# Weight casts behind the output gate's copies, a written TensorE order for the inverse and attention's output products, and query scaling on ScalarE

## The chip, the cores and the metric

One core of one Trainium2 chip runs the whole program. The time is the device time of one execution in microseconds (us). Of the kernel before there are three timed runs and one profiled execution, whose records the profile and the trace show.

## The reference, cut to what matters

One encoder layer on 512 tokens of width 1024: a feed-forward half step, a token mixer of two head groups, a second feed-forward half step, each behind an RMS norm with scale and shift from a condition vector. The change lies in the mixer:

```python
proj = h @ w_in                                    # q, k, v, z of the delta group; latents of attention
qkv = silu(causal_conv(concat(gq, gk, gv)))        # 4 taps
# gated delta rule, chunks of 64, per head:
M = I + where(strict, beta * (k k^T) * decay, 0)   # unit lower triangular
W = triangular_solve(M, [v * beta, k * beta * exp(G)])
# recurrence over chunks with a state S, then
o_a = rms(o_a) * norm_w * silu(gz)                 # the output gate z
# latent attention, 4 heads, block-causal:
q_nope = rms(q_nope) * w * scale ;  q_rope = rope(rms(q_rope)) * scale
o_b = rms(softmax(q k^T) v) * norm_w
x = x + gate2 * (concat(o_a, o_b) @ w_out)
```

All is float32. The dense products are each made of three products of two rounded parts: high x high, high x low, low x high.

## The kernel before

Activations lie feature-major, in eight tiles of 128 features x 512 tokens, each as a high and a low part. A weight unit is 128 output features x 1024 inputs. It is loaded by a DMA that SyncE issues (`load`, L118), cast to its high part on ScalarE (L193) and subtracted to its low part on VectorE (L198). There are four buffers for each of raw, high and low parts. `next_unit` (L260) prepares a unit ahead of the one that it hands out. `dense` (L270) makes, for each of eight input tiles, three products of 512 columns (L266 to L268) into one of three accumulators in PSUM (`psa`); all other products use five more PSUM tiles (`psb`).

A scheduler that works at compile time orders the instructions of each engine. It takes them by program order where its own model of time has their inputs ready, so an instruction can be placed ahead of one written before it. Each engine then works through its list in order and waits at an instruction whose inputs or buffers aren't ready. The code can pin an order: `follow` (L128) puts one instruction behind another on its engine, and `matmuls_in_order` (L144) chains all TensorE instructions of a block except those marked loose.

The mixer (L1909) interleaves generators. `Side.step` advances one of its open generators to its next `yield`. Three sides exist: `chain` (lifting the latents, keys of the delta rule, base blocks, inverses, solves), `deltas` (query parts of the delta rule) and `att` (preparing queries and keys, attention by 128-query blocks and head pairs). `dense_units` (L1208) runs four dense units each for k, q, v and the gate z and steps the sides between them. Each unit ends in a `finish`: for z a copy on ScalarE from the accumulator (L1921), later passed through SiLU.

The parts that the change and the prediction touch:

- `prep_q` (L1730): sums of squares of the queries, reciprocal roots (L182 to L189), rotary part on VectorE (L1206 `qrx`, L1830 to L1834, result `qro`), transposes on TensorE (L1768). Then eight GpSimd multiplications scale the other query part in place (L1776, recorded at L1206 as `upo`), and four transposed head tiles follow (L1725).
- `base_blocks` (L1492): 16x16 diagonal blocks of the inverse by substitution on VectorE, with two round trips through DRAM whose DMAs are in SyncE's queue beside the weight loads.
- `inverse` (L1533), one generator for each of four token blocks of 128: two steps of 128x128 products (L1553, L1559), two steps of 32x32 products in two halves j = 0 and 64 (L1569 with copies L1571, L1577 with L1579), a transposition (L1587), and two steps of 64x64 products (L1592, L1598).
- `solve` (L1605) uses an inverse; `recur` (L1637) carries the state through the four blocks; `gated_out` (L1681) norms and gates a block and writes the delta heads' tiles of `mixed`; `attended` (L1887) writes an attention head's tile of `mixed` (high part L1905, low part L1906).
- `out_attended` (L2036): the output projection's half that belongs to attention, for each of eight output tiles four slices, one for each head, of three products of 512 columns.
- The loop at L1992 runs until the second solve and `deltas` are done. It steps `chain` twice, `deltas` once, attention (`rest`) four times and, once attention is through, one slice of `out_attended` (`fill`). No order is pinned there. The loop over `recur` behind it already stands inside `matmuls_in_order`, with chain and attention loose.

Behind the mixer comes the second feed-forward step, in a pinned order.

Of the kernel before, what the change touches and what calls it, by code (L numbers as in the profile page):

```python
# [14 lines left out]
AF = mybir.ActivationFunctionType  # L15
# [3 lines left out]
P = 128  # L19
# [60 lines left out]
class Block:  # L80
# [1124 lines left out]
    def mul(self, out, a, b, eng=None):  # L1205
        (eng or self.nc.vector).tensor_tensor(out=out, in0=a, in1=b, op=ALU.mult)  # L1206

    def dense_units(self, n, side, steps, finish):  # L1208
        for i in range(n):
            u, p = self.next_unit(), self.acc()  # L1210
            for k in range(0, 8, 2):
                self.dense(p, u, self.h, k0=k, k1=k + 2)
                side.step(steps)
            finish(i, p)

    def latents(self, nb):

# [315 lines left out]
    def inverse(self, p):  # L1533

        nc = self.nc
        h4 = lambda x: x.rearrange("p (h d) -> p h d", h=4)
        hs = lambda h: slice(h * P, (h + 1) * P)
        at = self.at[p]

        def flip(src):  # L1540

            t = self.slot(s="T")
            nc.vector.transpose(out=t, in_=src)
            return t

        t = self.slot(s="t0")
        self.mul(t.rearrange("p (h i c) -> p h i c", h=4, i=8),
                 self.t16[:, 4 * p:4 * p + 4, :].unsqueeze(2).to_broadcast([P, 4, 8, 16]),
                 self.dmask.rearrange("p (i c) -> p i c", i=8).unsqueeze(1).to_broadcast([P, 4, 8, 16]))
        u = flip(t)  # L1550
        py = self.aux()
        for h in range(4):
            nc.tensor.matmul(py[:, hs(h)], at[:, hs(h)], t[:, hs(h)], start=True, stop=True)  # L1553
        y = self.slot(s="Y")
        self.mul(h4(y), h4(py), self.lmask.unsqueeze(1).to_broadcast([P, 4, P]))
        yield
        pz = self.aux()
        for h in range(4):
            nc.tensor.matmul(pz[:, hs(h)], y[:, hs(h)], u[:, hs(h)], start=True, stop=True)  # L1559
        un = self.slot(s="U")  # L1560
        nc.vector.tensor_tensor(out=un, in0=u, in1=pz, op=ALU.subtract)
        t = flip(un)
        yield

        py, y = self.aux(), self.slot(s="Y")
        for j in (0, 64):
            a, b = slice(j, j + 32), slice(j + 32, j + 64)
            for h in range(4):
                nc.tensor.matmul(py[b, 32 * h:32 * h + 32], at[a, h * P + j + 32:h * P + j + 64],  # L1569
                                 t[a, h * P + j:h * P + j + 32], start=True, stop=True, tile_position=(j, j + 32))  # L1570
            nc.scalar.copy(y[b, :P], py[b, :P])  # L1571
        yield
        pz = self.aux()
        for j in (0, 64):
            a, b = slice(j, j + 32), slice(j + 32, j + 64)
            for h in range(4):
                nc.tensor.matmul(pz[a, 32 * h:32 * h + 32], y[b, 32 * h:32 * h + 32],  # L1577
                                 un[b, h * P + j + 32:h * P + j + 64], start=True, stop=True, tile_position=(j + 32, j))
            nc.vector.tensor_scalar(out=h4(un[a, :])[:, :, j + 32:j + 64],  # L1579
                                    in0=pz[a, :P].rearrange("p (h c) -> p h c", h=4), scalar1=-1.0, scalar2=None,  # L1580
                                    op0=ALU.mult)
        yield

        a, b = slice(0, 64), slice(64, P)
        pt, t = self.aux(), self.slot(s="T")
        for h in range(4):
            nc.tensor.transpose(pt[a, 64 * h:64 * h + 64], un[a, h * P:h * P + 64], self.ident[a, a])  # L1587
        nc.scalar.copy(t[a, :256], pt[a, :256])
        yield
        py, y = self.aux(), self.slot(s="Y")  # L1590
        for h in range(4):
            nc.tensor.matmul(py[b, 64 * h:64 * h + 64], at[a, h * P + 64:h * P + P], t[a, 64 * h:64 * h + 64], start=True,  # L1592
                             stop=True, tile_position=(0, 64))
        nc.scalar.copy(y[b, :256], py[b, :256])
        yield
        pz = self.aux()
        for h in range(4):
            nc.tensor.matmul(pz[a, 64 * h:64 * h + 64], y[b, 64 * h:64 * h + 64], un[b, h * P + 64:h * P + P], start=True,  # L1598
                             stop=True, tile_position=(64, 0))
        nc.vector.tensor_scalar(out=h4(un[a, :])[:, :, 64:], in0=pz[a, :256].rearrange("p (h c) -> p h c", h=4),  # L1600
                                scalar1=-1.0, scalar2=None, op0=ALU.mult)
        yield
        self.inv[p] = un
# [77 lines left out]
    def gated_out(self, p):  # L1681

        nc = self.nc
        ss = self.small(4, "gs")
        self.head_squares(self.o[p], ss)
        ve = self.small(4, "ve")
        nc.vector.scalar_tensor_tensor(out=ve, in0=ss, scalar=1.0 / P, in1=self.oe[:, 4 * p:4 * p + 4], op0=ALU.mult,
                                       op1=ALU.add)
        r = self.rsqrt(ve, 4)
        yield  # L1690
        on = self.head_scale(self.o[p], r)
        yield
        j = self.vcol["gdn_norm_w"]
        pt = self.aux()
        for h in range(4):
            nc.tensor.transpose(pt[:, h * P:(h + 1) * P], on[:, h * P:(h + 1) * P], self.ident)
        m = self.slot(s="mf")
        ts = slice(p * P, (p + 1) * P)
        for h in range(4):
            hs = slice(h * P, (h + 1) * P)  # L1700
            mh, ml = self.mixed[h]
            nc.vector.scalar_tensor_tensor(out=m[:, hs], in0=pt[:, hs], scalar=self.cwT[:, j:j + 1],
                                           in1=self.zT[h][:, ts], op0=ALU.mult, op1=ALU.mult)
            nc.scalar.copy(mh[:, ts], m[:, hs])
            nc.vector.tensor_tensor(out=ml[:, ts], in0=m[:, hs], in1=mh[:, ts].bitcast(F32), op=ALU.subtract)
        yield

    def head_squares(self, o, ss):
# [21 lines left out]
    def prep_q(self, q):  # L1730

        nc = self.nc
# [3 lines left out]
        for b in range(NB):  # L1736
            for g in range(2):
                c = 6 * (2 * b + g)
# [11 lines left out]
        rqn, rqr = r[:, :16], r[:, 16:]  # L1750
# [21 lines left out]

        for b in range(NB):
            for g in range(2):
                qv = q[b][g][:, :384].rearrange("p (h d) -> p h d", h=2)[:, :, :128]
                self.mul(qv, qv, self.bc(rqn[:, 4 * b + 2 * g:4 * b + 2 * g + 2], 2), nc.gpsimd)  # L1776
        yield
        for h in range(4):
            c = (h % 2) * 192
# [129 lines left out]
    def mixer(self, nb):  # L1909
# [8 lines left out]

        def z_done(i, p):
            z = self.slot(s="z")  # L1920
            nc.scalar.copy(z, p)  # L1921
            self.zT.append(z)

        def conv_done(ct0, dst):
            def f(i, p):
# [6 lines left out]

        self.inv = [None] * NB
        self.kd, self.us, self.o, self.wk = ([None] * NB for _ in range(4))
        self.S = None

        def prepared():
            self.qrT, self.qnT, self.knT = [], [], []
# [36 lines left out]
                yield  # L1975

        chain.add(solving())
        self.dense_units(4, Rates(sides, (1, 0.75, 2)), 1, z_done)
        silu(self.zT)
        accum = self.slot(s="na")  # L1980

        fill = Side()
# [6 lines left out]

        rest = Side(wide=3)  # L1990
        rest.add(others())
        while self.wk[1] is None or deltas.open or deltas.todo:  # L1992
            chain.step(2)
            deltas.step()
            rest.step(4)
            if not rest.open and not rest.todo:
                fill.step(1)

        def loosely(side, n):
            with self.traced() as block:  # L2000
                side.step(n)
            self.loose.update(i.name for i in block)

        na = self.norm_half(0, accum, 6, True)
        self.mixed[:4] = [(self.slot(F32R, "mh"), self.slot(F32R, "ml")) for _ in range(4)]
        with self.matmuls_in_order():
            gated = Side(wide=NB)
            for p in range(NB):
                while self.wk[p] is None:
                    loosely(chain, 1)  # L2010
                for _ in self.recur(p):
                    loosely(chain, 2)
                    loosely(rest, 4)
                    if not rest.open and not rest.todo:
                        fill.step(3)
                    gated.step(2)
                gated.add(self.gated_out(p))
                gated.step()
                if p == 1:
                    def half():  # L2020
                        while len(gated.todo) + len(gated.open) > 2:
                            yield
                        yield from self.out_half(0, accum)
                    fill.add(half())
            while rest.open or rest.todo:
                loosely(rest, 1)
            fill.step(4)
            gated.flush()
            fill.flush()
            self.new_h()  # L2030
            self.tm = [self.slot(s="tm") for _ in range(KT)]
            drain(self.out_half(1, accum, na))
            drain(na)
# [72 lines left out]
```

## Time and profile before

| what | us |
|---|---|
| median of 3 runs | 1079.23 |
| lowest, highest | 1076.95, 1079.45 |
| the profiled execution | 1077.71 |
| its span, first to last instruction | 1076.0 |
| mean granted TensorE clock | 0.987 |

In the rows of the trace, a window row has for each engine its busy us and, in brackets, the number of instructions, then the granted TensorE clock as a share of full speed, the share of time in which the DMA engines worked, and GB/s. A timeline row has start and duration in us, the engine, the line of the kernel, the operation and what it writes and reads; in square brackets stands how long the engine was idle before it and what ended that. A float32 product of 128 or fewer columns appears as two records. PE is TensorE, DVE VectorE, ACT ScalarE, POOL GpSimd, SP SyncE.

### The profile page before, as it was taken

The numbers are of one execution on the slowest core, as the hardware profiler recorded it, in microseconds if no ns is written. First come the engines' busy times: TensorE is split into PE (matmuls) and PEld (weight loads), VectorE is DVE, ScalarE is ACT, GpSimd is POOL, SyncE is SP. The second block draws the span as 40 slices with busy tenths as digits, with TensorE's granted clock in tenths as the row PEclk, the third lists the DMA queues.
The fourth block names the chain that finished last, engine by engine and source line by source line (L and its number), as shares of the span: only waits on it lengthen the run. The fifth ranks groups of instructions, "written<-read, shape, count | busy, mean of one in ns | idle before, by whom it ended". The sixth has DMA issues, their size and how long they took to land. (4 is left out here: it accounts for less than half of the span.)

```text
span 1076.0 us, 15659 instructions
## 1 busy us (share of the span) xinstructions
PE 1046.7 (97%) x6183; PEld 899.1 (84%) x6183; DVE 689.4 (64%) x1231; ACT 445.3 (41%) x761; POOL 51.3 (5%) x103
## 2 busy tenths in 40 slices
PE   6999999999999999998999899999999999999998
PEld 5788878788887898887778578988899999999997
DVE  4488983433577445558868644769768787777633
ACT  3342222222222245566575363465534444444322
POOL 1000000000000011102000030220000000000000
PEclk8999999999999999999999898999999999999999
DMA  9989963233698349411203001153432333233222
GB/s 274 277 240 310 301 203 99 81 98 93 199 289 263 95 120 240 113 49 40 79 25 92 26 21 39 40 126 91 129 107 79 118 115 98 83 118 99 67 71 79
DMA packets 203687, 136.85 MB, mean 127 GB/s; under 512 B 13777, under 2 KB 186590, under 8 KB 203614
## 3 DMA queue, kind: packets, MB, share of 16 engines
q1 hardware_dynamic: 202318, 131.14, 41.1%
q0 software_dynamic: 1296, 4.72, 2.4%
q8 instruction: 48, 0.79, 0.3%
q14 instruction: 25, 0.20, 0.1%
HBM read 128.63 MB, written 2.49 MB: 122 GB/s over the span
## 5 line engine op out<-in xcount | busy, mean ns | idle before, releaser
L266 PE MATMUL pa<-hh,wh 128*128 128x512 f32 (+1 forms) x597 | 227.0, 380 | 4.3 <-ACT z L1921 4.3
L268 PE MATMUL pa<-hh,wl 128*128 128x512 f32 (+1 forms) x597 | 225.0, 377 | 2.7 <-DMA wl<-wr 2.7
L267 PE MATMUL pa<-hl,wh 128*128 128x512 f32 (+1 forms) x597 | 224.8, 377 | 0.0
L193 ACT CAST wh<-wr 128x1024 fp32r<-128x1024 f32 (+1 forms) x106 | 108.0, 1019 | 258.3 <-PE pa L267 184.4
L198 DVE TENSOR_TENSOR wl<-wr,wh 128x1024 fp32r<-128x1024 f32 (+1 forms) x97 | 114.4, 1180 | 99.0 <-ACT wh L193 94.5
L266 PE MATMUL pa<-ah,wh 128*128 128x512 f32 (+1 forms) x396 | 145.5, 367 | 0.6 <-DVE xT L873 0.4
L267 PE MATMUL pa<-al,wh 128*128 128x512 f32 (+1 forms) x396 | 144.5, 365 | 0.0
L268 PE MATMUL pa<-ah,wl 128*128 128x512 f32 (+1 forms) x396 | 143.5, 362 | 0.0
L266 PEld LDWEIGHTS pa<-hh,wh 128*128 128x128 f32 x597 | 113.6, 190 | 27.2 <-ACT z L1921 4.7
L268 PEld LDWEIGHTS pa<-hh,wl 128*128 128x128 f32 x597 | 113.5, 190 | 23.1 <-DMA wl<-wr 3.3
L267 PEld LDWEIGHTS pa<-hl,wh 128*128 128x128 f32 x597 | 113.5, 190 | 19.2 <-DVE hl L453 0.4
L268 PEld LDWEIGHTS pa<-ah,wl 128*128 128x128 f32 x396 | 74.8, 189 | 12.0
L266 PEld LDWEIGHTS pa<-ah,wh 128*128 128x128 f32 x396 | 75.2, 190 | 10.4 <-ACT wh L193 1.7
L267 PEld LDWEIGHTS pa<-al,wh 128*128 128x128 f32 x396 | 75.2, 190 | 7.2
L551 DVE SCALAR_TENSOR_TENSOR aa<-ar,sc,aa 128x512 f32<-128x512 f32 x98 | 73.2, 751 | 9.7 <-DMA ar<-in_w_ada 8.5
L846 PE MATMUL pb<-fh,wh 128*128 128x256 f32 x144 | 40.7, 282 | 0.0
L848 PE MATMUL pb<-fh,wl 128*128 128x256 f32 x144 | 40.7, 283 | 0.0
L848 PE MATMUL pb<-hh,wl 128*128 128x256 f32 x144 | 40.7, 283 | 0.0
L847 PE MATMUL pb<-fl,wh 128*128 128x256 f32 x144 | 40.7, 282 | 0.0
L847 PE MATMUL pb<-hl,wh 128*128 128x256 f32 x144 | 40.7, 282 | 0.0
L846 PE MATMUL pb<-hh,wh 128*128 128x256 f32 x144 | 40.6, 282 | 0.0
L873 DVE SCALAR_TENSOR_TENSOR xT<-pa,mod,xT 128x512 f32<-128x512 f32 (+1 forms) x40 | 29.4, 736 | 17.5 <-PE pa L268 17.5
(433 smaller groups left out, 1995.0 us busy)
## 6 DMA issues: line engine op xcount, KB each, us to landing
wr<-in_ffn_w_in SPq DMA_DIRECT2D x82, 512.0 KB, 4.1
ar<-in_w_ada SPq DMA_DIRECT2D x48, 512.0 KB, 5.9
wr<-in_ffn_w_out SPq DMA_DIRECT2D x34, 512.0 KB, 3.4
ar<-in_w_ada SPq DMA_DIRECT2D x48, 256.0 KB, 4.8
wr<-in_w_in SPq DMA_DIRECT2D x21, 512.0 KB, 3.9
wr<-in_ffn_w_out SPq DMA_DIRECT2D x17, 384.0 KB, 3.4
wl<-wr POOLq DMA_DIRECT2D x9, 512.0 KB, 5.6
wr<-in_w_out SPq DMA_DIRECT2D x8, 512.0 KB, 4.8
```

The costliest lines, as they stand in the source:

```text
L193: self.nc.scalar.copy(hi, raw)
L198: self.nc.vector.tensor_tensor(out=lo, in0=raw, in1=hi.bitcast(F32), op=ALU.subtract)
L266: mm(out, wh, xh, start=start, stop=False)
L267: mm(out, wh, xl, start=False, stop=False)
L268: mm(out, wl, xh, start=False, stop=stop)
L551: nc.vector.scalar_tensor_tensor(out=acc, in0=a, scalar=sc, in1=acc, op0=ALU.mult, op1=ALU.add)
L846: mm(out, wh, xh, start=start and k == 0, stop=False, **kw)
L847: mm(out, wh, xl, start=False, stop=False, **kw)
L848: mm(out, wl, xh, start=False, stop=stop and k == 3, **kw)
L873: nc.vector.scalar_tensor_tensor(out=self.xT[t][:, ts], in0=p[:, ts], scalar=gate[:, t:t + 1], in1=self.xT[t][:, ts], op0=ALU.mult, op1=AL ...
```

## The change

Four edits in the mixer, and one condition that goes with them.

1. For the gate's units, `dense_units` gets `tied=True`. Two units are prepared first. Each later unit is prepared after a gate copy is written, and its instructions on ScalarE (the cast) are pinned behind that copy. This holds the casts of the third and fourth gate unit and of the first two units of the output projection.
2. The loop at L1992 is put inside `matmuls_in_order`, with `deltas` and attention loose. It steps `chain` once a turn and `fill` every second turn, so that one slice of attention's output products stands after every two steps of the inverse, in an order that TensorE keeps.
3. In the inverse's 32x32 steps the two halves alternate product by product, and the two copies come after all eight products.
4. The queries are scaled by sixteen ScalarE activations of 128x128 with a column of factors, instead of eight GpSimd multiplications of 128x256.
5. The output projection's first half starts by a count of gated blocks (`self.gated`) instead of by the number of open generators.

```diff
-    def dense_units(self, n, side, steps, finish):
+    def dense_units(self, n, side, steps, finish, tied=False):
+        if tied:
+            self.prefetch(2)
         for i in range(n):
-            u, p = self.next_unit(), self.acc()
+            u, p = self.ready.pop(0) if tied else self.next_unit(), self.acc()
             for k in range(0, 8, 2):
                 self.dense(p, u, self.h, k0=k, k1=k + 2)
                 side.step(steps)
-            finish(i, p)
+            done = finish(i, p)
+            if tied:
+                with self.traced() as block:
+                    self.prefetch(2)
+                for x in block:
+                    if x.engine == done.engine:
+                        self.follow(x, done.name)
...
         py, y = self.aux(), self.slot(s="Y")
-        for j in (0, 64):
-            a, b = slice(j, j + 32), slice(j + 32, j + 64)
-            for h in range(4):
+        for h in range(4):
+            for j in (0, 64):
+                a, b = slice(j, j + 32), slice(j + 32, j + 64)
                 nc.tensor.matmul(py[b, 32 * h:32 * h + 32], at[a, h * P + j + 32:h * P + j + 64],
                                  t[a, h * P + j:h * P + j + 32], start=True, stop=True, tile_position=(j, j + 32))
+        for j in (0, 64):
+            b = slice(j + 32, j + 64)
             nc.scalar.copy(y[b, :P], py[b, :P])
...
         for b in range(NB):
             for g in range(2):
-                qv = q[b][g][:, :384].rearrange("p (h d) -> p h d", h=2)[:, :, :128]
-                self.mul(qv, qv, self.bc(rqn[:, 4 * b + 2 * g:4 * b + 2 * g + 2], 2), nc.gpsimd)
+                for e in range(2):
+                    qv, c = q[b][g][:, 192 * e:192 * e + P], 4 * b + 2 * g + e
+                    nc.scalar.activation(qv, qv, AF.Copy, scale=rqn[:, c:c + 1])
...
-        self.dense_units(4, Rates(sides, (1, 0.75, 2)), 1, z_done)
+        self.dense_units(4, Rates(sides, (1, 0.75, 2)), 1, z_done, True)
...
-        while self.wk[1] is None or deltas.open or deltas.todo:
-            chain.step(2)
-            deltas.step()
-            rest.step(4)
-            if not rest.open and not rest.todo:
-                fill.step(1)
...
+        with self.matmuls_in_order():
+            turn = 0
+            while self.wk[1] is None or deltas.open or deltas.todo:
+                chain.step(1)
+                loosely(deltas, 1)
+                loosely(rest, 4)
+                turn += 1
+                if not rest.open and not rest.todo and turn % 2:
+                    fill.step(1)
...
-                        while len(gated.todo) + len(gated.open) > 2:
+                        while self.gated < 2:
                             yield
```

The second 32x32 step (L1574 to L1581) is changed like the first. `z_done` returns its copy; `gated_out` counts up `self.gated` at its end.

More of the change, by code (lines that the diff above doesn't have):

```diff
@@ L1573, in inverse @@
         pz = self.aux()
-        for j in (0, 64):
-            a, b = slice(j, j + 32), slice(j + 32, j + 64)
-            for h in range(4):
+        for h in range(4):
+            for j in (0, 64):
+                a, b = slice(j, j + 32), slice(j + 32, j + 64)
                 nc.tensor.matmul(pz[a, 32 * h:32 * h + 32], y[b, 32 * h:32 * h + 32],
                                  un[b, h * P + j + 32:h * P + j + 64], start=True, stop=True, tile_position=(j + 32, j))
+        for j in (0, 64):
+            a = slice(j, j + 32)
             nc.vector.tensor_scalar(out=h4(un[a, :])[:, :, j + 32:j + 64],
@@ L1705, in gated_out @@
             nc.vector.tensor_tensor(out=ml[:, ts], in0=m[:, hs], in1=mh[:, ts].bitcast(F32), op=ALU.subtract)
+        self.gated += 1
         yield
@@ L1920, in z_done @@
             z = self.slot(s="z")
-            nc.scalar.copy(z, p)
+            done = nc.scalar.copy(z, p).ins
             self.zT.append(z)
+            return done
         def conv_done(ct0, dst):
@@ L1934, in mixer @@
         self.kd, self.us, self.o, self.wk = ([None] * NB for _ in range(4))
-        self.S = None
+        self.S, self.gated = None, 0
         def prepared():
```

## The prediction

> **What bounds the kernel now.** I read the page's busy shares and the granted clock first.
>
> ```profile
> span 1076.0 us, 15659 instructions
> PE 1046.7 (97%) x6183; PEld 899.1 (84%) x6183; DVE 689.4 (64%) x1231; ACT 445.3 (41%) x761; POOL 51.3 (5%) x103
> PEclk8999999999999999999999898999999999999999
> ```
>
> TensorE is busy in 97% of the span, so an edit on another engine pays only where TensorE stands still or where its clock is halved. The clock row dips twice in the second half, in slices that fall into the mixer. Next I read the waits of TensorE.
>
> ```profile
> PE pa L266 <- ACT z L1921: 4.3, 1, 4.3
> PE pb L1768 <- DVE qro L1834: 2.8, 2, 2.6
> ```
>
> Columns: total, times, longest. These are two of its three longest kinds of wait after the start, and both lie in code that the diff touches. Then I cut the mixer into stretches at the waits and the clock steps.
>
> ```profile
> core 0: us, PE busy (x) PEld busy (x) DVE busy (x) ACT busy (x) POOL busy (x), PEclk, DMA share, GB/s
> 596.30:600.60 4.30, 0.02 (x1) 0.00 (x0) 2.25 (x5) 4.23 (x8) 0.00 (x0) 0.77 0.22 58
> 600.60:605.50 4.90, 4.89 (x17) 4.22 (x18) 3.41 (x6) 0.59 (x1) 0.00 (x0) 0.50 0.16 56
> 605.50:628.70 23.20, 23.18 (x165) 17.58 (x164) 12.29 (x25) 11.69 (x29) 0.87 (x1) 1.00 0.01 2
> 637.00:643.00 6.00, 6.00 (x96) 4.53 (x95) 2.74 (x9) 3.44 (x8) 4.38 (x5) 1.00 0.01 3
> 643.00:653.20 10.20, 10.20 (x67) 8.74 (x68) 4.30 (x7) 2.15 (x4) 0.00 (x0) 0.50 0.00 0
> 664.40:690.00 25.60, 25.05 (x167) 22.11 (x167) 19.50 (x43) 11.24 (x28) 5.11 (x5) 1.00 0.14 42
> ```
>
> TensorE idles from 596.30 to 600.60, then runs 4.90 us at half clock. It is then full until 628.70. From 643.00 it runs 10.20 us at half clock again although it was 6.00 of 6.00 us busy just before: there it was busy with small products. After that it is full again, so time saved ahead of 690 reaches the end unless something else holds it.
>
> **The casts and the gate's copies.** The queue of ScalarE shows why TensorE idles.
>
> ```profile
> 596.12 1.05 ACT L193 CAST wh<-wr 128x1024 fp32r<-128x1024 f32 x1 [6.80 <-PE pa L267]
> ...
> 599.97 0.59 ACT L1921 COPY z<-pa 128x512 f32<-128x512 f32 x1
> ```
>
> ScalarE stands 6.80 us at a cast of a later weight, whose buffer a product still reads. The first gate copy is queued behind it. Three accumulators hold the first three gate units, so the fourth cannot start before 600.6. The edit puts each cast behind a gate copy, so this wait goes: 4.30 us, and of the 4.90 us at clock 0.50 half, 2.45, together 6.75.
>
> What is late next is the weight of the third gate unit, now cast only after the first copy.
>
> ```profile
> 597.20 1.22 DVE L198 TENSOR_TENSOR wl<-wr,wh 128x1024 fp32r<-128x1024 f32 x1 [0.33 <-ACT wh L193]
> 586.82 0.39 PE L266 MATMUL pa<-hh,wh 128*128 128x512 f32 x1
> ...
> 588.18 0.39 PE L266 MATMUL pa<-hh,wh 128*128 128x512 f32 x1
> ```
>
> Copy 0.59, cast 1.05, subtraction 1.22: 2.86 us. The cover is the second unit on TensorE: six products start in 588.18 - 586.82 = 1.36 us, 0.227 each, so 24 take 5.44. The slack is 2.6 us. But both engines work in order: behind a gate copy that waits for its unit stand softmax exponentials and latent copies, and behind one of those, waiting for VectorE, may stand the copy.
>
> ```profile
> 604.49 0.59 ACT L1871 COPY pT<-pb 128x512 f32<-128x512 f32 x1 [3.93 <-PE pb L1867]
> ```
>
> That wait of 3.93 us, in ScalarE's own order, is 1.3 over the slack. Between no new wait and the whole 6.75 back I take 1.5, about one such overrun, since most of these waits need not meet a copy; a loss would need both held gate weights to come late. Net gain 5.25. The loads move too: their SyncE queue also carries the base blocks' transposes through DRAM, and a load that waits for a raw buffer would hold them. The held casts free raw buffers later; I cost this at nothing while four raw buffers cover the two units ahead, and leave it inside the 6.75.
>
> **Queries on ScalarE.** Eight GpSimd multiplications become sixteen ScalarE ones.
>
> ```profile
> 490.80 5.62 POOL L1206 TENSOR_TENSOR upo<-upo,sq 128x256 f32<-128x256 f32 x8 [23.95 <-DVE sq L189]
> 491.25 2.17 DVE L1206 TENSOR_TENSOR qrx<-upo,sq 128x128 f32<-128x128 f32 x4
> 493.45 0.99 DVE L1830 TENSOR_TENSOR rt<-qrx,rope 128x512 f32<-128x512 f32 x1
> 494.36 1.58 DVE L1833 TENSOR_TENSOR rt<-qrx,rope 128x256 f32<-128x256 f32 x2
> 495.98 0.98 DVE L1834 TENSOR_TENSOR qro<-rt,rt 128x512 f32<-128x512 f32 x1
> 497.48 0.89 DVE L1206 TENSOR_TENSOR qrx<-upo,sq 128x128 f32<-128x128 f32 x4
> 498.40 0.69 DVE L1830 TENSOR_TENSOR rt<-qrx,rope 128x512 f32<-128x512 f32 x1
> 499.01 0.75 DVE L1833 TENSOR_TENSOR rt<-qrx,rope 128x256 f32<-128x256 f32 x2
> 499.87 0.69 DVE L1834 TENSOR_TENSOR qro<-rt,rt 128x512 f32<-128x512 f32 x1
> ```
>
> The same four steps stand twice: beside GpSimd they take 2.17 + 0.99 + 1.58 + 0.98 = 5.72 us, without it 0.89 + 0.69 + 0.75 + 0.69 = 3.02. So GpSimd costs VectorE 2.70 us, and TensorE's 2.6 us wait for qro lies right behind. It goes. The new work's price comes from a row of the same form.
>
> ```profile
> 670.31 1.14 ACT L1660 ACTIVATE o<-pb,eG 128x128 f32<-128x128 f32 x4 [1.80 <-PE pb L1658]
> 499.28 1.05 ACT L193 CAST wh<-wr 128x1024 fp32r<-128x1024 f32 x1 [5.59 <-PE pa L267]
> ```
>
> 16 x 1.14 / 4 = 4.6 us, within the 5.59 us that ScalarE stood idle before 499.28. If that cover is gone, a convolution's copy waits behind all 4.6 and the edit loses 4.6 - 2.6 = 2.0. GpSimd's queue only loses work. I take a gain of 2.4, bounds -2.0 and 2.6.
>
> **The written order.** In the loop after the gates, the diff issues one step of the inverse per turn and one slice of attention's output products (three of 512 columns) every second turn, and TensorE must keep that order. By the code, at loop entry the inverses stand inside their 32x32 steps; then come 12 slices among 19 inverse steps and the first solves. Before, the scheduler put slices wherever small products weren't ready. These rows count the first of a slice's three products.
>
> ```profile
> 628.70:637.00 8.30, 2.30 (x6) 1.12 (x6) 1.00 0.19 64
> 637.00:643.00 6.00, 0.90 (x2) 0.37 (x2) 1.00 0.01 3
> 643.00:653.20 10.20, 1.26 (x2) 0.66 (x2) 0.50 0.00 0
> ```
>
> Six slices in the first 8.30 us are about 18 x 0.227 = 4.1 us, half of the time, and the clock held. Two slices in 6.00 us are 1.4, 23%, and the clock fell. So wide products seem to hold the clock, not small ones. In the new order the 64x64 steps come in pairs, then a slice.
>
> ```profile
> 641.89 0.68 PE L1592 MATMUL pb<-T,at 64*64 64x64 f32 x8
> 642.49 0.49 PE L268 MATMUL pa<-mh,wl 128*128 128x512 f32 x1
> 642.91 1.90 PE L1592 MATMUL pb<-T,at 64*64 64x64 f32 x16
> 644.75 0.79 PE L267 MATMUL pa<-ml,wh 128*128 128x512 f32 x1
> ```
>
> Eight such records take 642.49 - 641.89 = 0.60 us at full clock, so two steps 1.2 beside 0.68 of slice: 36%, between 23% that fell and 50% that held. Worth of a held clock: at half, eight records take (644.75 - 642.91) / 2 = 0.92, 0.32 lost. The code has 4 inverses x 2 such steps x 4 heads, two records each, 64; all but eight ran behind 643 and lost 7 x 0.32 = 2.2 us. The stretch's wide products, three kinds of two or three, about 8, lose 0.227 each at twice their time, 1.8. Together 4.0. I take half, 2.0, bounds 0 and 4.0.
>
> [...]
>
> The order also takes something. Before, slices of the first two output tiles ran while the last heads were unfinished; only a tile's fourth slice needs the last head.
>
> ```profile
> 638.06 0.73 DVE L1906 SCALAR_TENSOR_TENSOR ml<-pb,cwT,mh 128x512 fp32r<-128x512 f32 x1
> ```
>
> That head lands at 638.8. In the written order the first tile's fourth slice must be issued before the second tile's three and before all 64x64 steps; no product of the inverse or of the output may pass it. The three slices, 9 x 0.227 = 2.0 us, are no filler any more. I charge 2.0, bounds 0 and 6.
>
> **The 32x32 steps.** Their products now alternate between two row groups, and the two copies come after all of them.
>
> ```profile
> L1577 PE MATMUL pb<-U,Y x64: 191/191/212, 637.1 to 641.3; 32*32 32x32 f32 x64
> 624.15 0.43 PE L1569 MATMUL pb<-T,at 32*32 32x32 f32 x8
> 624.52 0.50 PE L268 MATMUL pa<-hh,wl 128*128 128x512 f32 x1
> ```
>
> Eight records take 0.37 us; 64 of each of the two lines are 16 x 0.37 = 5.9. If alternating did nothing it is 0, if neighbours overlapped fully 2.9. I take 0.6, near the bottom, because what surely goes is a wait for a copy between halves, which other products cover; at worst a first copy starts 0.4 later. [...]
>
> The counter for the gated half only changes when a fill step may start; by the code that fill is still at attention's products then, so nothing.
>
> **Sum.** The span is 1076.0, the profiled execution 1077.71 with what lies around it. 1077.71 - 5.25 - 2.4 - 2.0 - 0.6 + 2.0 = 1069.5 for that execution. It lay 1.5 below the median of the runs shown, 1079.23, so the forecast for the median is 1071.0.
>
> **Rivals.**
> *The wait moves.* A held cast arrives late and TensorE idles as long as before, ahead of the third or fourth gate unit. For it: waits of 6.80 and 3.93 us in ScalarE's queue. Against: 2.6 us of slack. 5.25 is lost: 1074.7, as median 1076.2. This is no change, since 0.3%, or 3.2 us, is what a measurement of this kernel tells from none.
> *The written order blocks.* The last head still lands at 638.8, because attention's chain of exponentials and copies sets it. Then TensorE stands before the first tile's fourth slice and 5.25 + 2.4 + 0.6 = 8.25 us saved ahead are waited off. Behind it are 2.0 us of slices more than before, at half clock, so another 2.0, and the clock term gives 0. 1077.71 + 4.0 = 1081.7, median 1083.2, slower. It decides from about 8 us of wait at this slice. For it: before, 10 us passed between the gates' last products at 628.70 and that head. Against: TensorE is full from 605.50 to 628.70, so attention then waits for TensorE, and moves with it.
> *All goes well.* Clock held and small products overlapped: 2.0 and 2.3 more, 1065.2, median 1066.7. For it: the 36% may suffice.
>
> **Numbers.** Forecast 0.45 (own range 1067 to 1075, its two most doubtful terms of 2.0 either way), all well 0.17, wait moves 0.24, order blocks 0.14. Faster 0.62, same 0.24, slower 0.14. Low end: every upper bound, 1077.71 - 6.75 - 2.6 - 4.0 - 2.9 + 1.5 = 1063.0. High end: the moved wait with the order's charge at its bound, 1076.2 + 4.0 = 1080.2, so 1081; the blocked order, 0.14, is left out.
>
> **What would show it.** Right: no wait of TensorE for z over 1 us; casts behind the copies on ScalarE; qro's chain near 3.0 us and no 2.6 us wait; no stretch of 10 us at half clock around the 64x64 steps. Wrong: a new wait of TensorE for wh, wl or z in the gate units (first rival); a wait for the last heads' mh or ml at L266 to L268, with half clock behind it (second); the queries' scaling between a convolution's product and its copy; a second dip of the clock of the old length, which voids the 2.0.

## The result and the profile after

The change made the kernel slower: median 1088.36 us of five executions (1086.75 to 1091.33), beside 1079.23 of the kernel before in the same measurement (five, 1076.95 to 1082.87). The ratio is 1.0094, 95% interval 1.0075 to 1.0113. Forecast were 1071.0 and the range 1063 to 1081.

The profiled execution after took 1091.33 us. Its page, the lines that answer to those shown of before:

```profile
span 1089.6 us, 15667 instructions
PE 1054.3 (97%) x6183; PEld 903.7 (83%) x6183; DVE 688.1 (63%) x1231; ACT 448.2 (41%) x777; POOL 45.6 (4%) x95
PEclk8999999999999999999998877999999999999999
```

TensorE is as full as before, with 7.6 us more of busy time for the same 6183 instructions. Look at the clock row in the mixer and then at the waits of TensorE (total, times, longest):

```profile
PE pb L1914 <- DVE on L1206: 6.7, 3, 3.8
PE pb L1561 <- ACT wh L193: 5.1, 1, 5.1
PE pb L1561 <- DVE t L1206: 1.9, 1, 1.9
```

Neither z nor qro is among them any more. In their place stand waits for finished attention heads, the longest of them for the last, and two waits of a first product of the inverse. The profile puts the longer of these two down to a high weight part, wh; the section on why the prediction was wrong shows what ended it. Cut at the steps of the clock (columns as before):

```profile
590.65:607.75 17.10, 11.10 (x42) 9.32 (x43) 8.60 (x15) 4.89 (x9) 0.00 (x0) 0.50 0.10 31
607.75:627.60 19.85, 19.85 (x135) 15.06 (x135) 12.21 (x23) 10.28 (x24) 0.00 (x0) 1.00 0.09 27
627.60:637.40 9.80, 8.72 (x85) 6.33 (x83) 3.33 (x5) 5.01 (x13) 1.01 (x1) 1.00 0.19 57
637.40:641.85 4.45, 0.69 (x12) 0.55 (x14) 2.46 (x4) 0.48 (x3) 3.39 (x3) 1.00 0.00 0
641.85:669.20 27.35, 27.35 (x179) 20.20 (x178) 11.04 (x19) 8.48 (x15) 4.06 (x5) 0.50 0.19 59
669.20:700.00 30.80, 30.80 (x215) 27.93 (x214) 18.77 (x40) 12.35 (x28) 4.09 (x4) 1.00 0.18 51
```

Half clock lasts 17.10 us and then 27.35, together 13 times 3.42, the length of a single stretch in the kernel before (718.11 to 721.53 us, at 0.50 throughout). Before, it lasted 17.05 us in this part (summed over windows of 2.5 us from 580 to 700), 5 times 3.41. A stretch of 3.42 us at half clock costs, by estimate, at most 3.42 / 2 = 1.7 us, where TensorE is full. Eight more cost up to 13.7; the spans differ by 13.6. But the loss is not clock alone. TensorE's busy time grew by 7.6 us and its idle time by 6.0 (1089.6 - 1054.3 = 35.3, before 1076.0 - 1046.7 = 29.3); the waits for finished heads are 6.7 - 1.8 = 4.9 of that.

The two parts hang together. The 3.42 us ahead of the second fall, first here, then in the kernel before:

```profile
638.43:641.85 3.42, 0.69 (x12) 0.55 (x14) 1.52 (x1) 0.02 (x1) 3.39 (x3) 1.00 0.00 0
639.60:643.02 3.42, 3.42 (x43) 2.54 (x43) 0.78 (x4) 1.64 (x5) 1.78 (x2) 1.00 0.02 5
```

In the changed kernel the clock falls behind a wait, with TensorE busy 0.69 of 3.42 us; in the kernel before it fell with no idle time. After the fall it stays at half for 27.35 us although TensorE is busy in all of them.

One execution of the kernel without the order below, 1087.18 us, fell into a slower state and is left out of that kernel's row.

### The profile page after: what moved, and what is told of

It is laid out like the page before. It is cut to its first block, busy times and chain, and to the rows that moved or that the text cites. A ratio compares the mean times of both kernels' runs of the same rounds, so it can differ in the third digit from the quotient of the medians.

```text
span 1089.6 us, 15667 instructions
## 1 busy us (share of the span) xinstructions
PE 1054.3 (97%) x6183; PEld 903.7 (83%) x6183; DVE 688.1 (63%) x1231; ACT 448.2 (41%) x777; POOL 45.6 (4%) x95
```

## The experiments

All were timed beside the kernel before on their own chip. Two columns beside the ratio bear the reading. "Stretches" is the time at half clock between 580 and 700 us of the profiled execution, divided by 3.42. "At 0.997" is the time at one and the same clock: every execution has a mean granted clock, and a line through 237 executions, each kernel around its own mean, falls by 0.80 us for each 0.001 of clock and accounts for 87% of the scatter within the kernels. The column is each kernel's mean moved along that line. The kernel before stands there at 1070.2 to 1070.6 in four measurements; the standard error of an entry is 0.3 to 0.6. Where no execution comes near 0.997 the entry is an extrapolation: the whole change, at 0.973 to 0.978, is moved by 17 us, and one or two us cannot be told there.

| kernel | median (executions) | ratio, 95% interval | at 0.997 | stretches |
|---|---|---|---|---|
| before | 1078.34 to 1079.24 (18 to 29) | 1 | 1070.4 | 5 |
| whole change | 1088.36 (5) | 1.0094, 1.0075 to 1.0113 | 1071.8 | 13 |
| queries alone | 1071.16 (7) | 0.9938, 0.9915 to 0.9960 | 1067.2 | 5 |
| hold alone | 1084.95 (12) | 1.0022, 0.9995 to 1.0048 | 1072.9 | 9 |
| order alone | 1090.60 (5) | 1.0108, 1.0092 to 1.0124 | 1074.1 | 11 |
| 32x32 steps alone | 1069.62 (6) | 0.9922, 0.9905 to 0.9940 | 1068.7 | 2 |
| without the hold | 1085.83 (6) | 1.0054, 1.0033 to 1.0074 | 1070.7 | 11 |
| without the order | 1075.45 (11) | 0.9961, 0.9943 to 0.9978 | 1068.5 | 3 |
| order with slices free | 1078.40 (12) | 0.9988, 0.9964 to 1.0012 | 1070.2 | 8 |
| whole, slices free | 1072.06 (8) | 0.9952, 0.9932 to 0.9972 | 1068.1 | 6 |
| order, slice every turn | 1097.10 (4) | 1.0179, 1.0159 to 1.0199 | 1084.6 | 8 |
| hold, three weights | 1079.57 (12) | 1.0016, 1.0002 to 1.0030 | 1069.8 | 8 |
| queries, first z copy early | 1077.04 (12) | 0.9984, 0.9969 to 0.9999 | 1067.6 | 7 |
| queries and 32x32 | 1072.61 (12) | 0.9947, 0.9925 to 0.9968 | 1067.2 | 6 |
| both, first z copy early | 1075.38 (12) | 0.9981, 0.9966 to 0.9995 | 1066.0 | 7 |
| before, 32x32 with added work | 1083.38 (12) | 1.0039, 1.0024 to 1.0054 | 1079.5 | 2 |
| whole, with added work | 1103.49 (6) | 1.0201, 1.0165 to 1.0236 | 1092.6 | 8 |

The stretches are those of one execution and scatter with the times. Outside 580 to 700 us each profile has up to five more, which the column leaves out (the kernel before three, the whole change four). The ratio is over all executions of the row.

**Queries alone.** The diff at L1776 (before) and nothing else:

```diff
-                self.mul(qv, qv, self.bc(...), nc.gpsimd)
+                    nc.scalar.activation(qv, qv, AF.Copy, scale=rqn[:, c:c + 1])
```

> The kernel before with the queries' scaling on ScalarE alone. Theory A (each edit has its own effect, and this one only removes what GpSimd costs VectorE): TensorE's wait of 2.6 us for qro goes, all else moves up, 1.5 to 2.6 us faster than before, ratio 0.9976 to 0.9986. Theory B (the time saved is waited off later, at the first round trip of the base blocks through DRAM): no change, ratio 0.999 to 1.001, with a longer wait of TensorE near the gates.

Faster by 8.1 us, three times what the first theory gave. At one clock the gain is 3.2 (1070.4 to 1067.2), near the direct 2.6; the rest is a higher mean clock, 0.9909 beside 0.9857.

**Hold alone.** `dense_units` with `tied`, and `z_done`, as in the diff.

> The kernel before with the held casts alone. Theory A (the first gate copy is late because softmax exponentials stand before it on ScalarE, not because of the cast; the hold only takes the third gate unit away as cover): TensorE idles 8 to 10 us before the third gate unit instead of 4.3, and its clock is halved for longer, 3 to 8 us slower, ratio 1.003 to 1.007. Theory B (the cast was what the copy stood behind, and the written order alone makes the change slow): the wait shrinks, 3 to 5 us faster, ratio 0.995 to 0.997.

No gain: 2.5 slower at one clock (1070.4 to 1072.9). Five executions lie at 1075 to 1080 with a clock of 0.987 to 0.994, seven at 1084.9 to 1087.0 with 0.981 to 0.983. The profile has the same two waits as the whole change, 5.1 and 1.8, together less than the 8 to 10 expected.

**Order alone.** The loop and the counter `self.gated`, as in the diff.

> The kernel before with the written order of the inverse and attention's output products alone (and the count of gated blocks). Theory A: slices of the output no longer run while TensorE waits for the last head; an idle stretch of 4 to 6 us near there and a half clock of 20 us or more through the 64x64 steps, where before it was 10.2; 4 to 8 us slower, ratio 1.004 to 1.007. Theory B (the blocking is only a consequence of the held casts, which delay attention): the order alone holds the clock and is 0 to 3 us faster, ratio 0.997 to 1.000.

Slower by 11.4, more than the 4 to 8 expected and more than the whole change. Attention's last heads are waited for longer (total, times, longest):

```profile
PE pb L1901 <- DVE on L1206: 4.1, 3, 2.6
```

Before it was 1.8 in three, 0.9 the longest. Ten of the eleven stretches lie behind 630 us.

**Without the hold.** The other parts together.

> The changed kernel without the held casts; the other edits as in the change. Theory A: the hold's share, 3 to 8 us, comes back against the changed kernel, so 1 to 5 us slower than before, ratio 1.001 to 1.005. Theory B of the hold (it helps or does nothing): as slow as the changed kernel or slower, ratio 1.008 or more.

Still slower, by 6.6, outside both theories. The hold adds 2.5 (1085.83 to 1088.36).

**32x32 steps alone.** The two loops turned inside out, as in the diff.

> Only the 32x32 steps are changed: their products alternate between the two row groups and both copies come after all of them. Forecast's term: 0.6 us gained, so 1078.6, bounds 0 and 2.9. A rival, after the other runs: any change of order in this stretch moves the stretches at half clock, and the time moves with them by several us either way; then the mean clock of the run, and not the width of the two lines, tells the time. Told apart by the group of the 32x32 lines (191 ns of one before) and by the granted clock at 600 to 670 us.

The fastest kernel of the study. The two groups of products (busy us, then mean ns of one), first here, then before:

```profile
L1569 PE MATMUL pb<-T,at 32*32 32x32 f32 x64 | 1.6, 193 | 0.0
L1579 PE MATMUL pb<-U,Y 32*32 32x32 f32 x64 | 1.2, 192 | 0.0
```

```profile
L1569 PE MATMUL pb<-T,at 32*32 32x32 f32 x64 | 3.3, 193 | 0.0
L1577 PE MATMUL pb<-U,Y 32*32 32x32 f32 x64 | 2.4, 193 | 0.0
```

One record still takes 193 ns, but the busy time falls from 5.7 to 2.8: neighbours overlap in pairs, the full 2.9 that the forecast set as upper bound. At one clock 1.7 of it reaches the end. The larger gain is the fall of the clock at 643, which does not come: from 603 to 700 us the clock is full.

**Without the order.** Hold, 32x32 and queries.

> The whole change without the written order and its counter: held casts, alternated 32x32 steps, queries on ScalarE. Theory that the written order makes most of the loss and the hold the rest: 1068 to 1076, with five stretches of half clock or fewer and no wait for the last heads over 2 us. Rival, that the hold alone would do the same: 1083 or more, with nine stretches as in the hold alone.

Faster than before, and 12.9 under the whole change. The wait of 5.1 stands in this profile as well, and three stretches lie around it, none between 600 and 700 us. So the hold's wait is no more than a few us of the loss and the order carries most of it. Without the hold the order costs as much: 13.2 from the queries with the 32x32 steps (1072.61, below) to the kernel without the hold (1085.83). At one clock the two differences are only 3.3 and 3.5; the rest is a lower clock.

**Whole change, slices free; order, slices free.** One word is taken back in the loop:

```diff
-                    fill.step(1)
+                    loosely(fill, 1)
```

> The whole change with one word of the order taken back: the slices of attention's output products are free of it, the inverse's steps keep theirs. Without the whole order it was 1075.6, with it 1088.4. Theory that the loss is in the slices that stand in the order behind steps that are not ready, and in the half clock that follows: 1074 to 1079, five to eight stretches at half clock. Rival, that the inverse's own order is the loss: 1085 to 1090, eleven to thirteen stretches.

> The written loop with the inverse's steps alone in their order; the slices of attention's output products are free of it. Theory that the order keeps slices behind steps that are not ready: the waits for the last heads (2.6 in the order alone) go, 630 to 640 us is full again, and the time is 1079 to 1082. Rival, that the loss comes from the loop itself (one step of the inverse a turn instead of two, in order): 1086 or more, with the half clock at 640 to 668 as long as in the whole order.

1072.06 beside 1088.36: the slices' place in the order is the loss, not the inverse's own order, not the step of one instead of two. In the profile the wait for the last heads shrinks (longest 1.8 instead of 3.8), and half clock in the inverse from eight stretches to two:

```profile
640.00:648.00 8.00, 7.99 (x50) 5.10 (x43) 5.76 (x11) 5.03 (x9) 4.27 (x4) 0.57 0.30 84
648.00:670.00 22.00, 22.00 (x183) 19.56 (x182) 9.30 (x15) 8.26 (x15) 1.04 (x1) 1.00 0.21 66
```

With the order and counter alone and free slices the time is that of the kernel before, just under the expected 1079 to 1082, and its executions run from 1071.47 at a clock of 0.997 to 1081.96 at 0.984.

**Order, a slice every turn.** `and turn % 2` is left out, all else as in the order alone.

> The written order and its counter alone, with a slice behind every step of the inverse instead of every second; no work is added or left out. The same order with a slice every second turn: 1090.6, ten stretches at half clock from 630 on. Theory that the clock stays low because the mix holds too few wide products: the mix is now half wide or more, five stretches or fewer, 1079 to 1084. Rival, that the idle time ahead of the last heads and not the mix sets the clock: eight or more stretches and 1088 to 1094.

A miss on both sides. Between 625 and 700 us the stretches fall from ten to six, but three more stand at 716 to 726, where the order alone has none: nine in place of ten. So a richer mix is not shown to help the clock, and the time rises to 1097.1. The filler is spent earlier: from 652 to 670 us 29 products that read `mh` run, in the order alone 14, in the kernel before 18. Later it is missing at the recurrence and the gated output:

```profile
PE pb L1696 <- DVE on L1206: 5.7, 2, 4.4
PE pa L266 <- ACT z L1922: 4.3, 1, 4.3
PE pb L1901 <- DVE on L1206: 4.1, 3, 2.7
PE pb L1650 <- DVE S L1670: 3.0, 1, 3.0
```

In the kernel before the first of these was 0.4, the third 1.8, and the last is not among its waits: 10.6 us more of waiting. That is most of the 14 by which it stands above the kernel before at one clock.

**Hold with three weights.** `self.prefetch(3)` in the two places of `prefetch(2)`.

> The held casts alone, but with three weights cast ahead of the first gate unit instead of two. Theory that the hold took the third gate unit's 24 products away as cover: TensorE has them again, its idle time at 590 to 600 us falls from 5.1 to at most the 4.3 of the kernel before, and the time is 1077 to 1080. Rival, that the hold's loss is where the clock falls later on and not the cover: 1084 to 1087 in most executions, as with two weights (1084.95).

The wait of the inverse's product falls from 5.1 to 2.2, and at one clock the hold's loss goes (1072.9 to 1069.8). The third unit's products run again from 591.3 to 594.3, between the inverse's products. So what was missing was that unit as cover, for want of its weight. But nothing is gained over the kernel before.

**First z copy early, with the queries.** Casts not held. The side work of the first gate unit is issued behind its copy, and the softmax exponentials follow that copy:

```diff
                 self.dense(p, u, self.h, k0=k, k1=k + 2)
-                side.step(steps)
+                if not first or i:
+                    side.step(steps)
             finish(i, p)
+            if first and i == 0:
+                self.tabled = self.z0
+                for _ in range(4):
+                    side.step(steps)
```

> Queries on ScalarE, casts not held, and the side work of the first gate unit is issued behind that unit's copy, so that the copy stands ahead of the softmax exponentials in ScalarE's queue; nothing is left out. Theory that the copy waits for the exponentials: the wait of TensorE for z of 4.1 us goes with the half clock behind it, 4.1 + 2.4 = 6.5 under the queries alone (1071.2), so 1064.7. Theory of the forecast, that the cast in front of the copy is the holder: the cast still stands where it was, nothing changes, 1071. Third: TensorE waits at the same place for the first product of the inverse or for a weight instead; then the idle time at 590 to 600 stays at 4 us or more under another name, 1069 to 1072.

The copy now runs at 579.4 us and the wait for z is gone. Two windows of it, then of the queries alone:

```profile
585.00:600.00 15.00, 14.70 (x76) 11.70 (x75) 9.79 (x19) 7.75 (x14) 1.01 (x1) 1.00 0.36 87
600.00:610.00 10.00, 6.36 (x38) 4.58 (x38) 7.00 (x12) 2.25 (x7) 0.00 (x0) 0.96 0.18 55
```

```profile
585.00:600.00 15.00, 9.42 (x48) 7.16 (x47) 9.49 (x19) 7.37 (x14) 1.01 (x1) 0.96 0.36 89
600.00:610.00 10.00, 10.00 (x45) 7.77 (x45) 4.73 (x10) 1.00 (x3) 0.00 (x0) 0.71 0.01 2
```

TensorE fills 585 to 600 and then stands 3.64 us in the next ten, for the inverse's first factors (a wait for t of 3.9 in three). At one clock the two kernels are equal, 1067.6 and 1067.2. Of the readings in the expectation the third comes nearest: the wait moves, though by ten us, and the time lies above all three. By its median this kernel is 5.9 slower than the queries alone, with two stretches more.

**Queries and 32x32; both with the early copy.**

> The queries on ScalarE and the alternated 32x32 steps, nothing else. Each alone: 1071.2 and 1069.6. Theory that the time is that of full clock (1062 to 1068 in these profiles) plus about 1.7 us for each stretch of 3.4 us at half clock: the alternated steps leave two such stretches, the queries take 2.6 us of waiting away, so 1066 to 1068, with two stretches in the profile. Rival, that each gain is a chance of where the stretches fall and that together they fall as in the kernel before: 1073 or more, with five stretches or more.

> Queries on ScalarE, alternated 32x32 steps, and the first gate unit's copy issued ahead of the side work, so that it stands ahead of the softmax exponentials. Time at full clock, by the line through all executions: each of the three kernels it is made of stands at 1067 to 1069 for a mean clock of 0.997, so 1064 to 1066 there. Theory that the time then follows the stretches at half clock: with two of them 1066 to 1068, with six, as in two of the three, 1073 to 1075. If the copy's place were worth nothing even so: 1072.6 as without it.

Two gains that each stood alone do not add: 1072.61, its executions from 1067.46 at a clock of 0.996 to 1077.88 at 0.984, where the 32x32 steps alone keep 0.994 to 0.997. At one clock it is 1.5 better than they. The early copy gains 1.2 more at one clock and loses it through the clock. So no version of the study is shown to beat the 32x32 steps alone, at 0.9922.

**Added wide products.** The kernel before, and the whole change, with products of the identity that nobody reads, written beside the used columns of the same PSUM tile; in the first behind every four 32x32 products, in the second also behind every second 64x64 product:

```diff
+            nc.tensor.matmul(py[:, 256:], self.ident, at[:, :256], start=True, stop=True)
```

> The kernel before, with added work: behind every four 32x32 products one product of the identity with 256 columns, whose result nobody reads, 16 in all, about 0.26 us each (four such took 1.03), 4.2 us. Theory that the clock falls because small products fill a stretch although TensorE is busy: the three stretches at half clock after 643 us go, 5.1 us saved for 4.2 spent, 1077 to 1079 although work was added, and the granted clock is 1.00 from 630 to 660. Rival, that the clock falls by what went before or by the busy time: the fall stays, and the added work costs 4.2 to 8, 1083 to 1087.

> The whole change, with added work: one product of the identity with 256 columns behind every two pairs of 32x32 products and behind every second 64x64 product, 32 in all, 0.26 us each at full clock, 8.3 us; nobody reads their results. Theory that the half clock through the inverse is the price of the written order: the eight stretches from 640 to 668 go or shrink to two, about 10 to 13.6 us saved for 8.3 spent, 1083 to 1087. If the half clock stays for another reason, the added work costs 8.3 to 16.6: 1096 to 1105.

Both expectations took a product for 0.26 us, the time of a record; a float32 product is two records (the first kernel's 16 added products have 32 in its profile), so the added work is 16 x 0.52 = 8.3 and 32 x 0.52 = 16.6. In the first, TensorE does more and the clock at 643 holds:

```profile
637.00:650.00 13.00, 12.56 (x111) 7.95 (x109) 5.46 (x11) 3.84 (x7) 6.86 (x6) 1.00 0.13 42
650.00:660.00 10.00, 10.00 (x88) 7.60 (x86) 3.44 (x7) 2.88 (x6) 0.00 (x0) 1.00 0.01 2
```

Its time agrees: 1079.1 + 8.3 - 3 x 1.7 = 1082.3, measured 1083.38, and its mean clock over twelve executions is 0.992 beside 0.987. In the second the stretches in the inverse fall from eight to three, but it is 15.1 slower than the whole change and 20.8 at one clock, 4.2 more than the added work; that rest is not explained. The first agrees with a clock that falls for want of wide products while TensorE is busy. It does not prove it: added work also moves every later product, and the 32x32 steps alone keep the clock there with no wide product added. How large a share would be needed is not shown.

## Why the prediction was wrong

**The casts and the gate's copies** (5.25). The step that failed is "ScalarE stands 6.80 us at a cast of a later weight ... The first gate copy is queued behind it." True in the queue, wrong as a cause. Between cast and copy stand the softmax exponentials. In the two fences below they begin with a table load that waits for the first maximum (it starts within 0.1 us of that maximum's end). In the kernel before that maximum came at 595.88 + 0.42 = 596.30 and the table load, behind the cast, at 597.19: by the same wait the copy would have run, without the cast, some 0.8 earlier, not 4.3. The queries alone show it with the cast out of the way, at 590.57, and TensorE still idle for 4.1:

```profile
590.57 1.04 ACT L193 CAST wh<-wr 128x1024 fp32r<-128x1024 f32 x1 [0.20 <-PE pa L267]
...
595.68 0.42 DVE L1857 TENSOR_REDUCE mx<-pb 128x1 f32<-128x256 f32 x1
...
596.18 1.28 ACT L168 ACT_TABLE_LOAD   x1 [4.57 <-DVE mx L1857]
...
598.96 0.59 ACT L1922 COPY z<-pa 128x512 f32<-128x512 f32 x1
```

In the whole change the copy runs when it ran before, and the cast that was put behind it comes too late to give TensorE work in the gap:

```profile
590.66 0.69 DVE L1206 TENSOR_TENSOR t<-t,mk 128x512 f32<-128x512 f32 x1 [1.85 <-DMA t<-t_d]
591.50 2.05 PE L1561 MATMUL pb<-t,at 128*128 128x128 f32 x8 [1.92 <-DVE t L1206]
...
596.63 0.42 DVE L1870 TENSOR_REDUCE mx<-pb 128x1 f32<-128x256 f32 x1
...
597.14 1.28 ACT L168 ACT_TABLE_LOAD   x1 [9.73 <-DVE mx L1870]
...
599.92 0.59 ACT L1935 COPY z<-pa 128x512 f32<-128x512 f32 x1
600.07 0.75 DVE L1920 SCALAR_TENSOR_TENSOR ml<-pb,cwT,mh 128x512 fp32r<-128x512 f32 x1 [2.43 <-ACT mh L1919]
600.38 1.07 ACT L193 CAST wh<-wr 128x1024 fp32r<-128x1024 f32 x1
600.73 0.68 DVE L1206 TENSOR_TENSOR t<-t,mk 128x512 f32<-128x512 f32 x1
...
601.56 1.84 PE L1561 MATMUL pb<-t,at 128*128 128x128 f32 x7 [5.15 <-ACT wh L193]
```

The profile puts the last wait down to the cast, but the product that waits reads t and not wh. The cast ends at 600.38 + 1.07 = 601.45 and t at 600.73 + 0.68 = 601.41, 0.15 us ahead of the product; at 591.50 it was 0.15 as well (590.66 + 0.69 = 591.35). So t, read that way, ended the wait. It stands on VectorE behind a multiplication (`ml`) that waits for ScalarE's work behind the exponentials. With three weights the third unit needs no late cast and 2.2 us of the same wait are left.

The chain closes on itself: the maximum needs scores, the scores stand on TensorE behind the inverse's first product, that waits for t, and t for a DMA; meanwhile the third gate unit's 24 products, which ran in this gap before, have no weight. "The cover is the second unit on TensorE" counted 2.6 us of slack, and the copy came later than that. The first rival foresaw such a wait, with all of the 5.25 as its price; the forecast charged 1.5 for it. And a second step failed behind it, which the early copy shows: even with the wait gone, TensorE only waits elsewhere. 4.3 us of idle time counted as 4.3 us of gain.

**Queries on ScalarE** (2.4). Right in mechanism and size. The chain takes 0.89 + 0.69 + 0.75 + 0.69 = 3.02 us, and TensorE no longer waits for qro. The sixteen activations cost ScalarE 0.99 + 1.56 + 2.46 = 5.0 us, 4.6 forecast. In the whole change:

```profile
494.12 0.89 DVE L1206 TENSOR_TENSOR qrx<-upo,sq 128x128 f32<-128x128 f32 x4
495.05 0.69 DVE L1844 TENSOR_TENSOR rt<-qrx,rope 128x512 f32<-128x512 f32 x1
495.65 0.75 DVE L1847 TENSOR_TENSOR rt<-qrx,rope 128x256 f32<-128x256 f32 x2
496.44 0.69 DVE L1848 TENSOR_TENSOR qro<-rt,rt 128x512 f32<-128x512 f32 x1
```

**The 32x32 steps** (0.6). The direction was right and the size off: 2.9 of TensorE time (5.7 to 2.8 us of busy time, one record still at 193 ns), 1.7 at the end at one clock. The overlap, which the forecast took for its upper bound, came in full. The prediction left out that this edit may also keep the clock, as it does in the 32x32 steps alone, which was worth more.

**The written order** (a net charge of 0). This is the step that turned the forecast: a gain of 2.0 against a charge of 2.0, where the runs with and without the order differ by 12.9 and 13.2 us. "36%, between 23% that fell and 50% that held", of which half the 4.0 was taken, failed, and so did the weight of the second rival, 0.14. In the inverse the pattern came as forecast, two steps, then a slice:

```profile
655.40 1.97 PE L1604 MATMUL pb<-T,at 64*64 64x64 f32 x16
657.30 0.79 PE L266 MATMUL pa<-mh,wh 128*128 128x512 f32 x1
...
658.87 1.97 PE L1610 MATMUL pb<-U,Y 64*64 64x64 f32 x16
```

One period is 658.87 - 655.40 = 3.47 us, 1.97 of it small: 43% wide, at half clock for eight stretches. The share neither kept nor brought back the clock. And it came to be tested at the worst moment, because the order had taken the filler away:

```profile
641.16 0.63 PE L1914 MATMUL pb<-ident,on 128*128 128x128 f32 x4 [3.81 <-DVE on L1206]
641.72 0.99 PE L1587 MATMUL pb<-U,Y 32*32 32x32 f32 x32
642.64 0.80 PE L266 MATMUL pa<-mh,wh 128*128 128x512 f32 x1
```

The slices follow a 32x32 step that the scheduler placed behind the last head's transposes, although its factor `Y` was copied by 637.88 (637.35 + 0.53 for the copy at L1581). All slices waited, where the first ran at 628.9 before and six filled 628.70 to 637.00. Freeing the slices alone brings the whole change from 1088.36 to 1072.06. "The three slices ... are no filler any more, 2.0" counted three; it was all of them. The second rival's own condition also differs: it asked for a wait before the first tile's fourth slice, and its price of 4.0 had 2.0 us lost to half clock beyond the 10.20 us of before, where the profile has 27.35 us at half clock. Why the clock stays low that long stays open.

**The range** left out the blocked order and took the clock for a term of 4.0 at most, what the one fall without idle time seen before was worth.

## What to carry to other kernels

An engine's idle time is worth what the chain behind it gives back: before counting it, ask of each instruction between the suspected holder and its victim when its own inputs come. Here filler was worth most where the scheduler could put it; a written order that mixes filler with steps that can be late makes the filler late as well. Where the granted clock differs from one execution to the next, compare kernels at one clock and with many executions, and read a gain of one edit as a gain of that schedule, since two such gains need not add.

## What the runs showed of the hardware

In the profiles of the kernel before and of the changed one, time at half clock between 580 and 725 us came in stretches of 3.42 us or whole multiples of it: in the kernel before 6.83 us (598.67 to 605.50), 10.25 (643.02 to 653.27) and 3.42 (718.11 to 721.53), in the changed kernel 17.10 and 27.35, which are 5 and 8 times 3.42. In the single stretch at 718.11 products of 256 columns start (721.09 - 718.53) / 12 = 0.213 us apart, at full clock behind it (723.89 - 722.46) / 12 = 0.119. The fall at 641.85 us came behind 3.42 us of which TensorE was busy 0.69. Idle time does not account for the rest: the clock then stayed at 0.50 for 27.35 us with no idle time, and in the kernel before it fell at 643.02 behind 3.42 us with TensorE busy in all of them. That fall did not come when wide products were added among the small ones (1.00 from 637 to 660 us), nor with the 32x32 steps alone (full from 603 to 700). The same program, the order with slices free, took 1071.47 us at a clock of 0.997 in one execution and 1081.96 at 0.984 in another. What sets the length of a stretch, and what begins one, is not shown.
